# Transposing DMAs of the FFN issued by ScalarE, and the join of each chunk tied behind later work

## The chip, the cores and the metric

One core of a Trainium2 chip runs the program. Its engines are named as in the profile: PE (TensorE, matmul), PEld (TensorE's weight load), DVE (VectorE), ACT (ScalarE), POOL (GpSimd) and SP (SyncE, which here only issues DMAs). Each engine works through its own list of instructions in order and waits at semaphores for the others; ACT can issue DMAs too, on a queue of its own. The metric is the device time in microseconds (us) of one execution, lower is better; the median of 3 runs before is 962.99 us (962.33 to 964.85).

## What is computed

Two layers, each of FFN, mixer, FFN, with RMS norms around them, over 256 tokens of width 1024 in float32. The change touches the FFN alone, of which there are four.

```python
def _swiglu(h, w_in, w_out):
    gate, up = jnp.split(h @ w_in, 2, axis=-1)
    return (jax.nn.silu(gate) * up) @ w_out

def reference(x, ffn_w_in, ffn_w_out, norm_gains, mix_w_in, mix_w_out, ...):
    for l in range(DEPTH):
        g = norm_gains[l]
        h = _swiglu(_rmsnorm(x, g[0]), ffn_w_in[l, 0], ffn_w_out[l, 0])
        x = x + 0.5 * _rmsnorm(h, g[1])
        ...
        h = _swiglu(_rmsnorm(x, g[4]), ffn_w_in[l, 1], ffn_w_out[l, 1])
        x = x + 0.5 * _rmsnorm(h, g[5])
    return x
```

The hidden width 2816 is cut into 11 chunks (0 to 10) of 256.

## The kernel before

Products are made at float32 accuracy from three matmuls on rounded halves: a matrix is split into a high part (a copy rounded to fp32r) and a low part (the rest). Weights stream from HBM in pieces of 1 MB (tile `wr`, three buffers). Each half of a piece is cast by ACT (`wh`, L298) and subtracted by DVE (`wl`, L299); a load of the next piece can start when both halves of the piece in its buffer have been split. These two lines are most of what ACT and DVE do.

A plain chunk c of the FFN runs like this. Two pieces give the gate and up columns. PE multiplies them with the tokens' operands (`both`) into one PSUM bank for each of two token tiles (`pin` or `ptr`, in turn). ACT evacuates the gate half through silu (`sil`, L270), DVE multiplies it with the up half (`h`, L610). The output product needs the hidden values with the hidden index on the partitions, so they are transposed by a DMA: transposing DMAs work on 16-bit words, so ACT first copies the two 16-bit halves of each float apart (`planes`, L617), the DMA turns them (L619, issued by SP, written back over `h`), and DVE joins the halves again (`hT`, L625, the join). Then ACT and DVE split the joined values into `hh` and `hl` (L640, L641), and PE multiplies them with the chunk's third piece into the output banks (`bk`).

`STEPS` sets the order of the program: I is the input product of a chunk, O an output product, L a load of an output piece, S a part of the tokens' sums. The output product of chunk c stands behind the input product of chunk c + 1. P7 makes chunks 7 and 8 together with seven instead of eight products (`pair`, its two hidden tiles are `h` and `v`, each with its own planes and DMA). Chunk 9 is plain again. Chunk 10 is computed already turned (`in_turned`, L700 and L705; evacuated by `su`, L659 to L664, which ends in `hh` and `hl` of its own) and needs no DMA. The end of an FFN is then the output products of chunks 8, 9 and 10 (`END`), first for token tile 0, then for tile 1. So an FFN has ten transposing DMAs: seven for chunks 0 to 6, two for the pair, one for chunk 9.

The order in which the instructions of different steps stand on an engine is worked out by a scheduler while the program is built. It keeps dependences; `after(ins, others)` adds a tie, which makes an instruction stand behind others in that order without a semaphore, and `high_priority` moves work ahead. Waits at run time are for data and buffers alone, apart from that fixed order.

Of the kernel before, what the change touches and what calls it, by code (L numbers as in the profile page):

```python
# [19 lines left out]
U16 = mybir.dt.uint16  # L20
AF = mybir.ActivationFunctionType
ALU = mybir.AluOpType
# [6 lines left out]
NT = S // P  # L29
# [106 lines left out]
class _Trunk:  # L136
# [157 lines left out]
    def halved(self, raw):  # L294

        nc = self.nc
        lo, hi = self.half_tiles()
        ia = nc.scalar.activation(hi, raw, AF.Copy)  # L298
        iv = nc.vector.tensor_tensor(lo, raw, hi.bitcast(F32), op=ALU.subtract)  # L299
        for oa, ov in self.turns.pop(0) if self.turns else ():  # L300
            self.after(ia, [oa] if oa else [])
            self.after(iv, [ov] if ov else [])
        return hi, lo
# [303 lines left out]
    def ffn_hidden(self, pin, r, h):  # L607
        sil = self.t2("sil", (P, 256))
        self.func(sil, pin[:, 0:256], AF.Silu, scale=r)
        self.nc.vector.scalar_tensor_tensor(h, pin[:, 256:512], r, sil, op0=ALU.mult, op1=ALU.mult)  # L610

    def ffn_planes(self, h):


        nc = self.nc
        planes = self.t2("planes", (P, 2, 512), U16)
        nc.scalar.activation(planes, h.bitcast(U16).rearrange("p (n u) -> p u n", u=2), AF.Copy)  # L617
        turned = h.bitcast(U16).rearrange("p (b n) -> p b n", b=8)
        nc.sync.dma_start_transpose(turned, planes.rearrange("p u n -> p (u n)"))  # L619
        return turned  # L620

    def ffn_joined(self, turned):

        hT = self.t2("hT", (P, 2, 2, P))
        self.nc.vector.tensor_copy(hT.rearrange("p a b n -> p (a b n)").bitcast(U16).rearrange("p (n u) -> p u n", u=2),  # L625
                                   turned.rearrange("p (u b) n -> p u (b n)", u=2))
        return hT

    def ffn_split(self, hs):
# [47 lines left out]
    def ffn(self, pre, gi_post):  # L677
        xT, r = pre
# [26 lines left out]
                            self.nc.tensor.matmul(b[:, 0:NT * P], self.cols(w[kh], k)[1][:, c], both[kh][:, k, 0:NT].rearrange("p i t -> p (i t)"),  # L705
                                                  start=False, stop=kh == 1 and k == 3, skip_group_check=True)

        def ready(c, h):
            hT = self.ffn_joined(self.ffn_planes(h.rearrange("p t j -> p (t j)")))
            return self.ffn_split([hT[:, t] for t in range(NT)])  # L710

        def chunk(c, pins):
            h = self.t2("h", (P, NT, 256))
            for t in range(NT):
                self.ffn_hidden(pins[t], r[t], h[:, t])
            hs[c] = ready(c, h)

        def product(b, x, w, new):
            for k in range(4):
                for n, (st, mv) in enumerate(((x[0], 0), (x[0], 1), (x[1], 0))):  # L720
                    self.nc.tensor.matmul(b, st[:, k, :], self.cols(w, k)[mv], start=new and k == n == 0,  # L721
                                          stop=k == 3 and n == 2, skip_group_check=True)

        def pair(c):


            tt, stt = self.nc.vector.tensor_tensor, self.nc.vector.scalar_tensor_tensor
            w = self.pair_blocks()
            b1, b2, b3, b4 = self.bank_pin(), self.bank_pin(), self.bank_tr(), self.bank_tr()
            s1, s2, s3, s4 = sums  # L730
            ahead = self.tc.high_priority
            p1, sil, u, v, h0 = self.t2("p1"), self.t2("sil"), self.t2("u"), self.t2("v"), self.t2("h")
            product(b1, xT[0][0], w["P1"], True)
            with ahead():
                self.nc.scalar.activation(p1, b1, AF.Copy)
            product(b4, s1, w["P5"], True)
            product(b2, s2, w["P6"], True)
            with ahead():
                tt(u, b2, p1, op=ALU.subtract)
            product(b3, s3, w["P7"], True)  # L740
            with ahead():
                tt(v, u, b3, op=ALU.subtract)
                tt(v, v, b4, op=ALU.add)
            product(b1, xT[0][1], w["P2"], False)
            with ahead():
                self.func(sil, b1, AF.Silu, scale=r[0])
            product(b4, s4, w["P3"], False)
            with ahead():
                tt(h0, b4, u, op=ALU.add)
                stt(h0, h0, r[0], sil, op0=ALU.mult, op1=ALU.mult)  # L750
            with ahead():
                turned = [self.ffn_planes(h0)]
            product(b3, xT[1][1], w["P4"], False)
            with ahead():
                tt(u, b3, u, op=ALU.subtract)
                self.func(u, u, AF.Silu, scale=r[1])
                stt(v, v, r[1], u, op0=ALU.mult, op1=ALU.mult)
                turned.append(self.ffn_planes(v))
            hT = [self.ffn_joined(v) for v in turned]
            for j in range(2):  # L760
                hs[c + j] = self.ffn_split([h[:, j] for h in hT])

        hs, po, wo = {}, [], {}
        if not xT:

            xT += [[], []]
            pins = [self.bank_bk() for _ in range(NT)]
            self.piece_at = 2
            with self.tc.manual_schedule(engines={mybir.EngineType.PE, mybir.EngineType.Activation, mybir.EngineType.DVE}):
                self.first_chunk(pins, xT)  # L770
            self.turns = [[(self.cast, self.split)]]
            for t in range(NT):
                ss = self.small("ss", (P, 2))
                for hf in range(2):
                    self.after(self.square(t, hf, ss), [self.cast])
                r.append(self.rsqrt_sum(ss, EPS))
            chunk(0, pins)
            w1 = [self.piece(), self.piece()]
            wo[0] = self.piece()
            pins = [self.bank_pin() for _ in range(NT)]  # L780
            for kh in range(2):
                for t in range(NT):
                    in_piece(t, kh, pins[t], w1[kh])
            chunk(1, pins)
        else:

            w0 = [self.piece(), self.piece()]
            w1 = [self.piece()]
            pa, pa1 = self.bank_pin(), self.bank_pin()
            in_piece(0, 0, pa, w0[0])  # L790
            in_piece(0, 1, pa, w0[1])
            h = self.t2("h", (P, NT, 256))
            self.ffn_hidden(pa, r[0], h[:, 0])
            yield "second"
            in_piece(0, 0, pa1, w1[0])
            pb = self.bank_pin()
            in_piece(1, 0, pb, w0[0])
            in_piece(1, 1, pb, w0[1])
            yield "running"
            w1.append(self.piece())  # L800
            in_piece(0, 1, pa1, w1[1])
            self.ffn_hidden(pb, r[1], h[:, 1])
            hs[0] = ready(0, h)
            wo[0] = self.piece()
            pb1 = self.bank_pin()
            h = self.t2("h", (P, NT, 256))
            self.ffn_hidden(pa1, r[0], h[:, 0])
            in_piece(1, 0, pb1, w1[0])
            in_piece(1, 1, pb1, w1[1])
            self.ffn_hidden(pb1, r[1], h[:, 1])  # L810
            hs[1] = ready(1, h)
        both, swap = list(self.both), 0
        tokens = self.pair_tokens(both)
        for at, step in enumerate(STEPS):
            kind, c = step[0], int(step[1:])
            if kind == "P":
                pair(c)
            elif kind == "S":
                sums = next(tokens)
            elif kind == "L":  # L820
                if wo.get(c) is None:
                    wo[c] = self.piece()
            elif kind == "I":
                if c == 3:
                    g = self.load_gpost(gi_post)
                    yield "middle"
                ws = [self.piece(), self.piece()]
                for later in STEPS[at + 1:]:
                    if later[0] != "L":
                        break  # L830
                    wo[int(later[1:])] = self.piece()
                if c == END[-1]:
                    break
                pins = [self.bank_pin() if swap else self.bank_tr() for _ in range(NT)]
                swap = 1 - swap
                for kh in range(2):
                    for t in range(NT):
                        in_piece(t, kh, pins[t], ws[kh])
                chunk(c, pins)
            else:  # L840
                if not po:
                    po = [[self.bank_bk() for _ in range(2)] for _ in range(NT)]
                for t in range(NT):
                    out_part(c, t, hs[c], wo[c])
# [572 lines left out]
```

## Time and profile before

| | us |
|---|---|
| median of 3 runs | 962.99 |
| the profiled execution | 960.19 |
| span of the profiled execution, first to last instruction | 958.4 |
| lowest and highest of the 3 runs | 962.33, 964.85 |

| stretch of the profiled execution (us from the span's start) | what runs |
|---|---|
| 0 to 180 | FFN 1 of layer 1 |
| 180 to 290 | mixer of layer 1 |
| 290 to 475 | FFN 2 of layer 1, the second FFN of the four |
| 475 to 655 | FFN 1 of layer 2, the third |
| 655 to 765 | mixer of layer 2 |
| 765 to 958 | FFN 2 of layer 2, the fourth |

How to read the rows: a group of instructions has its line in the kernel, the engine, the operation, the tiles `out<-in` (buffer numbers left out), and the shapes. In the timeline a row begins with the start and the length in us; a bracket at the end is the time that the engine sat idle before, and what ended it. Matmuls overlap, so a row's length is not the spacing of matmuls; the difference of two starts is. A row of waits gives who waited for whom, the sum in us, how often and the longest. A row of windows gives the stretch, its length, and then the busy time of PE, PEld, DVE, ACT and POOL in it, each with the number of instructions, the granted clock of PE (1.00 is all of it), the busy share of the DMA engines and GB/s. DMA issues are not counted as busy time of the engine that issues them.

### The profile page before, as it was taken

What the parts mean: (1) busy time and instruction counts of PE and PEld (TensorE: products, weight loads), DVE (VectorE), ACT (ScalarE), POOL (GpSimd) and SP (SyncE); (2) the same over time, 40 slices, a digit from 0 to 9 for tenths busy, and PEclk for the clock granted to TensorE, in tenths of its full rate; (3) what the DMA queues carried; (4) which work ended last, traced back from release to release, by engine and by line L of the source; (5) the groups of instructions that cost most, each with busy time, mean ns of one, the idle gap of its engine ahead of it and who ended that gap; (6) DMA issues with size and microseconds to landing.
All of it is one profiled execution on the core that took longest, in us unless ns stands there. A gap on an engine that the chain in (4) does not pass through costs nothing.

```text
span 958.4 us, 12128 instructions
## 1 busy us (share of the span) xinstructions
PE 943.1 (98%) x4475; PEld 779.5 (81%) x4475; DVE 739.2 (77%) x1069; ACT 597.3 (62%) x973; POOL 30.2 (3%) x55
## 2 busy tenths in 40 slices
PE   9999999999999999999899999999999999999997
PEld 6888888888878888887788888888878888888885
DVE  7786986788858975786699669867888588759864
ACT  8666556578756755565476656664769466656652
POOL 2100000000010000000000000000000100000000
PEclk9999999999999999999999999999999999999999
DMA  8896477346342875467449663763454338754741
GB/s 309 277 305 233 138 280 209 129 138 239 142 163 91 307 244 189 147 256 211 181 147 306 187 219 139 291 204 133 173 200 147 118 132 273 275 193 142 271 119 45
DMA packets 69882, 189.34 MB, mean 198 GB/s; under 512 B 45274, under 2 KB 46426, under 8 KB 49086
## 3 DMA queue, kind: packets, MB, share of 16 engines
q1 hardware_dynamic: 69246, 187.95, 58.1%
q8 instruction: 35, 0.57, 0.2%
q10 hardware_dynamic: 576, 0.61, 0.2%
q14 instruction: 25, 0.20, 0.1%
HBM read 177.01 MB, written 1.05 MB: 186 GB/s over the span
## 4 chain that ended last, share of the span: by engine, by line
PE 84%; DVE 6%; ACT 4%; DMA 4%; issue 2%; POOLq 0%; ACTq 0%; DVEq 0%
PE pin L483 10%; PE pin L485 10%; PE pin L484 10%; PE bk L485 9%; PE bk L484 9%; PE bk L483 9%; PE ptr L484 5%; PE ptr L485 5%; PE ptr L483 5%; PE ptr L721 4%; DVE wl L299 3%; PE pin L721 3%; DMA wr<-in_w_dram 2%; ACT wh L298 2%; DMA h<-planes 2%
## 5 line engine op out<-in xcount | busy, mean ns | idle before, releaser
L299 DVE TENSOR_TENSOR wl<-wr,wh 128x1024 fp32r<-128x1024 f32 x324 | 388.0, 1219 | 82.1 <-ACT wh L298 81.1
L298 ACT ACTIVATE wh<-wr 128x1024 fp32r<-128x1024 f32 x324 | 331.5, 1054 | 130.7 <-DMA wr<-in_w_dram 60.6
L483 PE MATMUL pin<-wh,both 128*128 128x512 f32 x496 | 195.9, 396 | 0.0
L485 PE MATMUL pin<-wh,both 128*128 128x512 f32 x496 | 193.2, 390 | 0.0
L484 PE MATMUL pin<-wl,both 128*128 128x512 f32 x496 | 193.1, 390 | 0.0
L483 PE MATMUL bk<-wh,hh 128*128 128x512 f32 x352 | 135.3, 391 | 2.5 <-ACT hh L640 2.5
L484 PE MATMUL bk<-wl,hh 128*128 128x512 f32 x352 | 136.9, 389 | 0.0
L485 PE MATMUL bk<-wh,hl 128*128 128x512 f32 x352 | 135.0, 390 | 0.8 <-DVE hl L641 0.8
L485 PEld LDWEIGHTS pin<-wh,both 128*128 128x128 f32 x496 | 93.1, 188 | 19.8
L483 PEld LDWEIGHTS pin<-wh,both 128*128 128x128 f32 x496 | 93.3, 188 | 19.3 <-issue 0.7
L484 PEld LDWEIGHTS pin<-wl,both 128*128 128x128 f32 x496 | 93.3, 188 | 18.1
L483 PEld LDWEIGHTS bk<-wh,hh 128*128 128x128 f32 x352 | 66.1, 188 | 16.6 <-ACT hh L640 3.0
L485 PEld LDWEIGHTS bk<-wh,hl 128*128 128x128 f32 x352 | 66.1, 188 | 15.3 <-DVE hl L641 1.6
L484 PEld LDWEIGHTS bk<-wl,hh 128*128 128x128 f32 x352 | 66.1, 188 | 13.4
L484 PE MATMUL ptr<-wl,both 128*128 128x512 f32 x192 | 74.7, 389 | 0.0
L485 PE MATMUL ptr<-wh,both 128*128 128x512 f32 x192 | 74.7, 389 | 0.0
L483 PE MATMUL ptr<-wh,both 128*128 128x512 f32 x192 | 73.4, 389 | 0.0
L640 ACT ACTIVATE hh<-hT 128x256 fp32r<-128x256 f32 x80 | 29.1, 407 | 43.4 <-DVE hT L625 41.9
L625 DVE COPY hT<-h 128x1024 uint16<-128x1024 uint16 x36 | 27.3, 757 | 34.9 <-DMA h<-planes 34.9
L617 ACT ACTIVATE planes<-h 128x1024 uint16<-128x1024 uint16 x36 | 37.8, 1050 | 11.9 <-DVE h L610 11.9
L483 PEld LDWEIGHTS ptr<-wh,both 128*128 128x128 f32 x192 | 36.0, 188 | 7.5
L484 PEld LDWEIGHTS ptr<-wl,both 128*128 128x128 f32 x192 | 36.0, 188 | 7.5
(247 smaller groups left out, 1229.1 us busy)
## 6 DMA issues: line engine op xcount, KB each, us to landing
wr<-in_w_dram SPq DMA_DIRECT2D x162, 1024.0 KB, 5.0
gpost<-in_gpost_dram SPq DMA_DIRECT2D x6, 512.0 KB, 6.1
wr<-in_w_dram SPq DMA_DIRECT2D x2, 512.0 KB, 6.2
wr<-in_w_dram SPq DMA_DIRECT2D x3, 256.0 KB, 4.5
x<-in_x_dram SPq DMA_DIRECT2D x3, 256.0 KB, 4.9
h<-planes SPq DMA_TRANSPOSE x36, 4.7
out_dram<-x SPq DMA_DIRECT2D x2, 256.0 KB, 2.1
x<-in_x_dram SPq DMA_DIRECT2D x2, 128.0 KB, 3.0
```

The costliest lines, as they stand in the source:

```text
L298: ia = nc.scalar.activation(hi, raw, AF.Copy)
L299: iv = nc.vector.tensor_tensor(lo, raw, hi.bitcast(F32), op=ALU.subtract)
L483: mm(ps, xh, wh, start=start, stop=False)
L484: mm(ps, xh, wl, start=False, stop=False)
L485: mm(ps, xl, wh, start=False, stop=stop)
L617: nc.scalar.activation(planes, h.bitcast(U16).rearrange("p (n u) -> p u n", u=2), AF.Copy)
L625: self.nc.vector.tensor_copy(hT.rearrange("p a b n -> p (a b n)").bitcast(U16).rearrange("p (n u) -> p u n", u=2), turned.rearrange("p (u ...
L640: self.nc.scalar.activation(hh, h, AF.Copy)
L721: self.nc.tensor.matmul(b, st[:, k, :], self.cols(w, k)[mv], start=new and k == n == 0, stop=k == 3 and n == 2, skip_group_check=True)
```

## The change

Three things are changed in the FFN's code; nothing that is computed differs.

1. The transposing DMA (L619) is issued by ACT, on ACT's queue, instead of SP.
2. A chunk's planes and its DMA (`send`) are separated from its join and split (`ready`). The join of chunk c is written behind the evacuation of chunk c + 1 and tied to stand behind its first hidden multiply. For the chunk ahead of the pair the tie is to the pair's first subtraction (`u`).
3. The joins of the pair are tied to stand behind a DVE split of chunk 9's first weight piece (`cut`), and chunk 9's join behind one of chunk 10's first piece.

```diff
@@ halved
         iv = nc.vector.tensor_tensor(lo, raw, hi.bitcast(F32), op=ALU.subtract)
+        self.cut = iv
@@ ffn_hidden
-        self.nc.vector.scalar_tensor_tensor(h, pin[:, 256:512], r, sil, op0=ALU.mult, op1=ALU.mult)
+        return self.nc.vector.scalar_tensor_tensor(h, pin[:, 256:512], r, sil, op0=ALU.mult, op1=ALU.mult)
@@ ffn_planes
-        nc.sync.dma_start_transpose(turned, planes.rearrange("p u n -> p (u n)"))
+        nc.scalar.dma_start_transpose(turned, planes.rearrange("p u n -> p (u n)"))
@@ ffn_joined
-    def ffn_joined(self, turned):
+    def ffn_joined(self, turned, others=()):
...
+        self.after(i, others)
         return hT
@@ ffn
-        def ready(c, h):
-            hT = self.ffn_joined(self.ffn_planes(h.rearrange("p t j -> p (t j)")))
-            return self.ffn_split([hT[:, t] for t in range(NT)])
+        def send(c, h):
+            sent[c] = self.ffn_planes(h.rearrange("p t j -> p (t j)"))
+
+        def ready(c, others):
+            if c in sent:
+                hT = self.ffn_joined(sent.pop(c), others)
+                hs[c] = self.ffn_split([hT[:, t] for t in range(NT)])

         def chunk(c, pins):
             h = self.t2("h", (P, NT, 256))
-            for t in range(NT):
-                self.ffn_hidden(pins[t], r[t], h[:, t])
-            hs[c] = ready(c, h)
+            i = [self.ffn_hidden(pins[t], r[t], h[:, t]) for t in range(NT)]
+            send(c, h)
+            ready(c - 1, i[:1])
@@ pair
             with ahead():
-                tt(u, b2, p1, op=ALU.subtract)
+                i = tt(u, b2, p1, op=ALU.subtract)
+            ready(c - 1, [i])
...
-            hT = [self.ffn_joined(v) for v in turned]
+            sent["pair"] = c, turned
+
+        def pair_ready(others):
+            c, turned = sent.pop("pair")
+            hT = [self.ffn_joined(v, others) for v in turned]
             for j in range(2):
                 hs[c + j] = self.ffn_split([h[:, j] for h in hT])
@@ second to sixth phase, first chunks
-            hs[0] = ready(0, h)
+            send(0, h)
...
-            self.ffn_hidden(pb1, r[1], h[:, 1])
-            hs[1] = ready(1, h)
+            i = self.ffn_hidden(pb1, r[1], h[:, 1])
+            send(1, h)
+            ready(0, [i])
@@ steps, kind "I"
-                ws = [self.piece(), self.piece()]
+                ws = [self.piece()]
+                cut = self.cut
+                ws.append(self.piece())
+                if "pair" in sent:
+                    pair_ready([cut])
...
                 if c == END[-1]:
+                    ready(c - 1, [cut])
                     break
```

What follows are rows of the instruction order at the end of the second FFN, where chunks 7 to 10 finish. The numbers belong to buffers of that place; a tile has another number in the two programs when more tiles were named ahead of it. Tiles `h_3833` and `v_3832` (after: `h_3823` and `v_3822`) are the pair, `h_4102` is chunk 9, `su_4255` and `su_4268` are chunk 10.

ACT before, from the planes of the pair:

```order
L617 ACTIVATE planes_3913<-h_3833 128x1024
L617 ACTIVATE planes_3931<-v_3832 128x1024
L298 ACTIVATE wh_4159<-wr_4156 128x1024
L270 ACTIVATE sil_4103<-pin_4052,rs_560_2886 128x256
L298 ACTIVATE wh_4169<-wr_4166 128x1024
L298 ACTIVATE wh_4163<-wr_4156 128x1024
L640 ACTIVATE hh_3938<-hT_3934 128x256
L270 ACTIVATE sil_4106<-pin_4053,rs_585_2973 128x256
L650 ACTIVATE rows_4179<-ptr_4176 128x256
L640 ACTIVATE hh_3940<-hT_3936 128x256
L640 ACTIVATE hh_3946<-hT_3934 128x256
L640 ACTIVATE hh_3948<-hT_3936 128x256
```

ACT in the change, from the same planes:

```order
L618 ACTIVATE planes_3913<-h_3823 128x1024
L618 ACTIVATE planes_3931<-v_3822 128x1024
L620 DMA_TRANSPOSE h_3823<-planes_3913 128x8x128
L620 DMA_TRANSPOSE v_3822<-planes_3931 128x8x128
L270 ACTIVATE sil_4103<-pin_4052,rs_560_2886 128x256
L298 ACTIVATE wh_4153<-wr_4146 128x1024
L298 ACTIVATE wh_4159<-wr_4156 128x1024
L270 ACTIVATE sil_4106<-pin_4053,rs_585_2973 128x256
L652 ACTIVATE rows_4179<-ptr_4176 128x256
L298 ACTIVATE wh_4288<-wr_4281 128x1024
L642 ACTIVATE hh_4026<-hT_4022 128x256
L642 ACTIVATE hh_4028<-hT_4024 128x256
```

Before, casts of weights stand between the planes and the evacuations; in the change both planes are followed at once by the issues of both transposing DMAs, and the evacuation `sil_4103` of chunk 9's first bank stands behind the issues. The evacuation `sil_4106` stood behind `hh_3938`, which needs the pair's first join; now it stands ahead of the first `hh`.

DVE before, from the join of chunk 9:

```order
L625 COPY hT_4112<-h_4102 128x2x512
L641 TENSOR_TENSOR hl_4115<-hT_4112,hh_4114 128x256
L299 TENSOR_TENSOR wl_4172<-wr_4166,wh_4173 128x1024
L641 TENSOR_TENSOR hl_4117<-hT_4112,hh_4116 128x256
L299 TENSOR_TENSOR wl_4283<-wr_4281,wh_4284 128x1024
L299 TENSOR_TENSOR wl_4424<-wr_4422,wh_4425 128x1024
L660 TENSOR_TENSOR su_4255<-pin_4181,su_4255 128x256
L660 TENSOR_TENSOR su_4255<-pin_4182,su_4255 128x256
L661 TENSOR_TENSOR su_4255<-su_4255,rows_4179 128x256
L299 TENSOR_TENSOR wl_4428<-wr_4422,wh_4429 128x1024
L660 TENSOR_TENSOR su_4268<-ptr_4183,su_4268 128x256
L661 TENSOR_TENSOR su_4255<-su_4255,rows_4179 128x256
```

DVE in the change, from the same join:

```order
L626 COPY hT_4166<-h_4102 128x2x512
L299 TENSOR_TENSOR wl_4162<-wr_4156,wh_4163 128x1024
L643 TENSOR_TENSOR hl_4169<-hT_4166,hh_4168 128x256
L299 TENSOR_TENSOR wl_4283<-wr_4281,wh_4284 128x1024
L643 TENSOR_TENSOR hl_4171<-hT_4166,hh_4170 128x256
L299 TENSOR_TENSOR wl_4424<-wr_4422,wh_4425 128x1024
L299 TENSOR_TENSOR wl_4428<-wr_4422,wh_4429 128x1024
L662 TENSOR_TENSOR su_4255<-pin_4181,su_4255 128x256
L662 TENSOR_TENSOR su_4268<-ptr_4183,su_4268 128x256
L662 TENSOR_TENSOR su_4268<-ptr_4184,su_4268 128x256
L662 TENSOR_TENSOR su_4255<-pin_4182,su_4255 128x256
L299 TENSOR_TENSOR wl_4434<-wr_4432,wh_4435 128x1024
```

The join (`hT_4112`, after `hT_4166`) stands at the same place among DVE's work, ahead of the second split of chunk 9's output piece (4156, before 4166), those of pieces 4281 and 4422 and the sums of chunk 10. Right behind it now stands a weight split (`wl_4162`) that does not need it; the adds of chunk 10 stand together.

SP before, the loads and transposing DMAs at this place:

```order
L291 DMA wr_4042<-in_w_dram 128x2048
L291 DMA wr_4146<-in_w_dram 128x2048
L291 DMA wr_4156<-in_w_dram 128x2048
L291 DMA wr_4166<-in_w_dram 128x2048
L619 DMA_TRANSPOSE h_3833<-planes_3913 128x8x128
L619 DMA_TRANSPOSE v_3832<-planes_3931 128x8x128
L291 DMA wr_4281<-in_w_dram 128x2048
L291 DMA wr_4422<-in_w_dram 128x2048
L619 DMA_TRANSPOSE h_4102<-planes_4109 128x8x128
L291 DMA wr_4432<-in_w_dram 128x2048
```

SP in the change:

```order
L291 DMA wr_4042<-in_w_dram 128x2048
L291 DMA wr_4136<-in_w_dram 128x2048
L291 DMA wr_4146<-in_w_dram 128x2048
L291 DMA wr_4156<-in_w_dram 128x2048
L291 DMA wr_4281<-in_w_dram 128x2048
L291 DMA wr_4422<-in_w_dram 128x2048
L291 DMA wr_4432<-in_w_dram 128x2048
L291 DMA wr_4442<-in_w_dram 128x2048
```

The three transposing DMAs are gone from between the loads; the loads stand in the same order (pieces 4136, 4146 and 4156 of the change are 4146, 4156 and 4166 of before).

More of the change, by code (lines that the diff above doesn't have):

```diff
@@ L618, in ffn_planes @@
         turned = h.bitcast(U16).rearrange("p (b n) -> p b n", b=8)
-        nc.sync.dma_start_transpose(turned, planes.rearrange("p u n -> p (u n)"))
+        nc.scalar.dma_start_transpose(turned, planes.rearrange("p u n -> p (u n)"))
         return turned
-    def ffn_joined(self, turned):
+    def ffn_joined(self, turned, others=()):
         hT = self.t2("hT", (P, 2, 2, P))
-        self.nc.vector.tensor_copy(hT.rearrange("p a b n -> p (a b n)").bitcast(U16).rearrange("p (n u) -> p u n", u=2),
-                                   turned.rearrange("p (u b) n -> p u (b n)", u=2))
+        i = self.nc.vector.tensor_copy(hT.rearrange("p a b n -> p (a b n)").bitcast(U16).rearrange("p (n u) -> p u n", u=2),
+                                       turned.rearrange("p (u b) n -> p u (b n)", u=2))
+        self.after(i, others)
         return hT
@@ L758, in pair @@
                 turned.append(self.ffn_planes(v))
-            hT = [self.ffn_joined(v) for v in turned]
+            sent["pair"] = c, turned
+        def pair_ready(others):
+            c, turned = sent.pop("pair")
+            hT = [self.ffn_joined(v, others) for v in turned]
             for j in range(2):
                 hs[c + j] = self.ffn_split([h[:, j] for h in hT])
-        hs, po, wo = {}, [], {}
+        hs, po, wo, sent = {}, [], {}, {}
         if not xT:
```

## The prediction

> **What bounds the kernel now.** I read the page's busy shares first, then PE's own waits, then the windows round the four FFN ends, where this change works.
>
> ```profile
> PE 943.1 (98%) x4475; PEld 779.5 (81%) x4475; DVE 739.2 (77%) x1069; ACT 597.3 (62%) x973; POOL 30.2 (3%) x55
> PE bk L483 <- ACT hh L640: 2.5, 1, 2.5
> PE ptr L1039 <- DVE y L1302: 1.8, 2, 1.1
> PE ptr L1039 <- DVE ra L1224: 1.2, 1, 1.2
> PE ptr L700 <- ACT wh L298: 0.9, 1, 0.9
> PE bk L485 <- DVE hl L641: 0.8, 1, 0.8
> 126.00:176.00 50.00, 50.00 (x238) 41.91 (x237) 37.75 (x53) 30.48 (x45) 0.00 (x0) 1.00 0.75 245
> 423.00:473.00 50.00, 45.74 (x214) 37.44 (x213) 33.77 (x49) 27.05 (x42) 0.00 (x0) 1.00 0.76 237
> 600.00:651.00 51.00, 51.00 (x241) 42.52 (x240) 39.25 (x54) 30.86 (x44) 0.00 (x0) 1.00 0.72 246
> 892.00:942.00 50.00, 50.00 (x238) 41.93 (x237) 35.35 (x51) 27.41 (x41) 0.00 (x0) 1.00 0.52 167
> ```
>
> TensorE (PE) is busy almost without a break, at full granted clock. The waits of L1039 lie in the mixer, which the change leaves alone; the other three are all in one place, the end of the second FFN (423 to 473 us). The ends of the other three FFNs show PE busy 50.00 of 50.00, 51.00 of 51.00 and 50.00 of 50.00. So whatever DMA waits the change removes elsewhere, only the second FFN's end can pay. The matmuls there give the prize:
>
> ```profile
> 444.36 0.63 PE L700 MATMUL ptr<-both,wh 128*128 128x512 f32 x2
> 445.87 0.73 PE L700 MATMUL ptr<-both,wh 128*128 128x512 f32 x2 [0.88 <-ACT wh L298]
> 465.91 0.39 PE L484 MATMUL bk<-wl,hh 128*128 128x512 f32 x1
> 466.14 0.39 PE L485 MATMUL bk<-wh,hl 128*128 128x512 f32 x1
> 469.06 0.50 PE L483 MATMUL bk<-wh,hh 128*128 128x512 f32 x1 [2.53 <-ACT hh L640]
> 469.39 0.40 PE L484 MATMUL bk<-wl,hh 128*128 128x512 f32 x1
> 470.64 0.50 PE L485 MATMUL bk<-wh,hl 128*128 128x512 f32 x1 [0.85 <-DVE hl L641]
> ```
>
> Starts follow each other at 466.14 - 465.91 = 0.23 us when nothing is missing. Two from 444.36 should have been followed at 444.82, not 445.87 (1.05 lost); 466.14 by 466.37, not 469.06 (2.69); 469.39 by 469.62, not 470.64 (1.02). Together **4.76 us**: no gain beyond this is in sight, 0.5% of the run.
>
> What made them late? The chain of waits over 436 to 472 us, and ACT's and SP's rows there:
>
> ```profile
> 436.85 8.49 DMA h<-planes
> 451.28 5.90 DMA h<-planes
> 460.80 4.76 DMA wr<-in_w_dram
> 465.59 1.07 ACT wh L298
> 438.10 1.06 ACT L617 ACTIVATE planes<-v 128x1024 uint16<-128x1024 uint16 x1 [1.27 <-DVE v L757]
> 447.20 0.74 DVE L625 COPY hT<-v 128x1024 uint16<-128x1024 uint16 x1
> 450.20 1.06 ACT L617 ACTIVATE planes<-h 128x1024 uint16<-128x1024 uint16 x1 [0.24 <-DVE h L610]
> 457.27 0.76 DVE L625 COPY hT<-h 128x1024 uint16<-128x1024 uint16 x1 [4.97 <-DMA h<-planes]
> 458.15 0.42 ACT L640 ACTIVATE hh<-hT 128x256 fp32r<-128x256 f32 x1 [6.89 <-DVE hT L625]
> 462.58 0.63 ACT L659 ACTIVATE su<-pin 128x256 f32<-128x256 f32 x2
> 436.85 2.37 SPq L619 DMA_TRANSPOSE h<-planes  x1
> 439.56 4.05 SPq L619 DMA_TRANSPOSE v<-planes  x1
> 443.73 6.06 SPq L291 DMA_DIRECT2D wr<-in_w_dram  x2
> ```
>
> Chunk 9's transposing DMA lands 5.90 us after its issue. DVE's join (hT) stands there 4.97 us and ACT's hh behind it 6.89 us, each with weight splits queued behind it. Those splits free the buffer of a load, which starts only at 460.80 and lands 4.76 later, and the last chunk's su operations stand behind its split. Chunk 10 thus reaches PE 2.69 us late.
>
> **The change part by part.** (1) *Forty transposing DMAs go from SP to ACT.*
>
> ```profile
> L619 SPq DMA_TRANSPOSE h<-planes x36: 1231/1232/2696, 29.3 to 923.7; - x36
> L619 SPq DMA_TRANSPOSE v<-planes x4: 1232/1336/4055, 148.7 to 915.6; - x4
> DMA to landing us min/median/max: 2.7/4.8/8.5
> 320.00:370.00 50.00, 50.00 (x223) 41.38 (x222) 36.94 (x50) 31.38 (x43) 0.00 (x0) 1.00 0.76 247
> 25.00:65.00 40.00, 40.00 (x178) 33.14 (x177) 33.05 (x46) 28.52 (x42) 2.62 (x3) 1.00 0.89 288
> ACT wh L298 <- DMA wr<-in_w_dram: 8.7, 4, 2.6
> ```
>
> Each costs ACT an issue. No row shows a transpose issued by ACT; the nearest are SP's, 1.23 us at the median and 4.05 at the worst. I take 1.23: 40 x 1.23 = 49 us more on ACT, which was busy 597.3. Among plain chunks that is some 3 x 1.23 = 3.7 us in the 50 from 320 on, where ACT was busy 31.4 and PE never waited: hidden, costing nothing while ACT stays well under 50. In the crowded first part (25 to 65 us) ACT goes from 28.5 to about 32 of 40; it had waited 8.7 us for weights between 30 and 60, and that idle time covers the issues. Without such cover one issue in front of a cast costs up to 1.23.
>
> (2) *SP is rid of them.* At 436.85 and 439.56 they held SP's queue for 2.37 and 4.05 us, and the load behind left at 443.73. Loads now leave as their buffers come free. Where PE had no wait that buys nothing; at the second FFN's end it takes the late weights away.
>
> (3) *Landing.* A transpose no longer stands behind an earlier load in SP's queue, but loads may now overtake it. Bounds: 2.7 to 8.5 us from issue; I take the median, 4.8.
> The Trainium skill (DMA: Bandwidth & Descriptors, Queues, rings and completion order) says that each DMA engine takes turns between the queues that have work, a packet at a time; the row of 8.49 us, a transpose issued while loads were landing, fits standing behind them, and by that rule a transpose on a queue of its own would land nearer 2.7, all 4.76 would go, and the sum would be -4.3 where the median gives -3.5. The same page (Rules for kernel authors) says that spreading DMAs over issuing engines brings no bandwidth, it only saves issue time; by that the landing would stay at 5.90, which the third rival below prices.
>
> (4) *The joins are tied later.* Chunk c's join (0.76) and split now follow the next chunk's evacuation. Its product is a whole chunk further on, so on PE's path this costs nothing. While the join waits for nothing, DVE's weight splits no longer queue behind a landing. The last ones can't be moved so far: chunks 7 and 8 are tied to a weight split of chunk 9, chunk 9 to one of chunk 10, and all three are needed at the end.
>
> (5) *The second FFN's end, step by step.* planes of v still ends at 438.10 + 1.06 = 439.16. ACT then issues h (to 440.4) and v (to 441.6), so h leaves 2.3 us later than before. v, issued at 440.4, lands at 445.2, its join stood at 447.20: 2.0 sooner. Chunk 9's planes move from 450.20 to some 448.2 and end at 449.3; DMA of 4.8: 454.1, against 457.2. In the new DVE order the second half of that chunk's weights is split right behind the join, so the load behind it can leave at 454.1 + 0.76 + 1.22 = 456.1 instead of 460.80, and lands at 460.8 instead of 465.56. From that landing to PE's 469.06 it took 3.5 us: 464.3. The su operations can't begin before their banks: 462.58 less the lost 1.05 is 461.5 at the latest, and the fourth FFN shows their length without a late load:
>
> ```profile
> 933.87 0.38 ACT L659 ACTIVATE su<-pin 128x256 f32<-128x256 f32 x1 [3.25 <-PE pin L705]
> 938.34 0.51 ACT L640 ACTIVATE hh<-su 128x128 fp32r<-128x128 f32 x2 [1.85 <-PE bk L484]
> ```
>
> There 938.34 - 933.87 - 1.85 of waiting for a bank = 2.6 us to hh, or 4.5 with it. So hh is ready between 464.3 and 466.0, and PE without its first loss wants it at 466.37 - 1.05 = 465.32. Left over: 0 to 0.7, and up to the 1.02 of hl. With a transpose of 2.7 all 4.76 go; with 8.5 each way none do. I take **-4.0**.
>
> (6) *The other ends.* The third FFN has the same order, planes of h and v ahead of both issues; its h leaves later, its v about when it did. The first and fourth keep h's issue ahead of v's planes, with two weight casts now between planes and issue of v. I allow **+0.5** for one of them to reach PE; 0 if shorter landings cover it, some 2 if not.
>
> Sum: -4.0 + 0.5 = -3.5 us. The profiled execution took 960.19 (span 958.4 and 1.8 around it): 956.7. The median of the runs shown is 962.99, 2.8 above it, so the forecast in those terms is **959.5**.
>
> **The rivals.**
> *A: the wait only changes its name* (0.25). Something else of the same chain, say the weight split that now stands ahead of the su products in DVE's order, keeps chunk 10 as late as it was, or small stalls at the other ends give the gain back. For it: all of DVE's work there is still there, and the third end has no margin that I can show. Against: 5 us of DVE idle time stood in that chain. Time: 963, 961 to 965.
> *B: slower, ACT is held by its own issues* (0.14). In the second and third FFN two transposes stand back to back on ACT. If the second blocks, as SP's did (4.05), ACT's evacuations, which SP's hold never touched, stand still for 2.37 + 4.05 - 2 x 1.23 = 4.0 us more than I counted. It decides where v's issue takes over some 3 us, because the banks' evacuation and chunk 9's planes follow it directly. The second FFN then gains nothing, the third loses up to 4.0: 963.0 + 4.0 = 967. Against it: SP's queue was full of loads then, ACT's holds transposes alone.
> *C: nothing lands sooner* (0.11). Loads run ahead on SP's queue and share the DMA engines, which were 0.76 busy at that end. With 5.90 for chunk 9 in place of 4.8 the chain of (5) ends 1.1 later, hh at 465.4 to 467.1: 0.1 to 1.7 left over and the 1.02 of hl, so a gain of 2.0 to 3.6, less the 0.5: about 960.7.
>
> **How the numbers follow.** Forecast 0.50, A 0.25, B 0.14, C 0.11. The forecast's own range is 958.0 to 961.0 (4.76 gone and nothing new: 958.2; 2 left over: 961). A difference under about 0.3% (2.9 us) can't be told from none with a few runs. Faster by more: most of the forecast's half and a little of C, 0.47. Within: the rest of it, C and A's most, 0.40. Slower: B less its mild end, 0.13. The range runs from 957.5 (all of the prize, and a little from runs that waited longer than the profiled one) to 966.0, which leaves out B's far end and little of A.
>
> **What would show it.** Right: PE's waits for hh L640, hl L641 and wh L298 at 440 to 475 us fall from 4.3 to under 1; PE stays busy throughout at the other three ends; SP no longer shows issues of 2 to 4 us; the last join waits under 4 us; ACT's issues take about 1.23. Wrong: an issue of 3 us or more on ACT ahead of sil or planes; new PE waits for wh, wl or hh at 25 to 65 us, in the pair, or at the third end; landings over 6 us at the median. What would also upset it is that the unprofiled runs lose time elsewhere: they are 2.8 above the profiled one, and if that lies in DMA waits the gain could be larger.

## The result, and the profile after

The changed kernel takes 991.93 us (median of 6 runs, 985.66 to 1006.89) against 962.83 before (also of 6 runs by now): the ratio is 1.0304, 95% interval 1.0252 to 1.0356. One of the six runs, 1006.89, lies over 1.5% above the fastest of them and is left out of the ratio. The change is slower by 3%, far above the range of the prediction (957.5 to 966.0). The profiled execution took 992.38, its span is 990.5: 32.1 more than before.

From the page of the changed kernel, the busy times, and from its waits of PE and DVE (sum in us, how often, the longest):

```profile
PE 953.4 (96%) x4475; PEld 786.0 (79%) x4475; DVE 738.8 (75%) x1069; ACT 598.1 (60%) x973; POOL 29.1 (3%) x55
PE bk L484 <- ACT hh L642: 22.6, 5, 9.9
DVE hT L626 <- DMA h<-planes: 55.8, 9, 12.6
```

PE's wait for `hh`, 2.5 us in one place before, is now 22.6 in five, and behind it stand DVE's joins, waiting 55.8 us for transposing DMAs in 9 places (34.9 in 23 before). PE is also busy 10.3 us longer (953.4 against 943.1) with the same matmuls. So of the 32.1 us, 21.8 are more idle time and 10.3 longer matmul time. The transposes themselves, from the view of the tile `planes` (issue time in ns min/median/max, first and last start):

```profile
L620 ACTq DMA_TRANSPOSE h<-planes x36: 1247/1249/3355, 31.1 to 955.6; - x36
L620 ACTq DMA_TRANSPOSE v<-planes x4: 1249/1813/4497, 162.4 to 939.4; - x4
DMA to landing us min/median/max: 2.7/6.5/19.3
```

The median landing went from 4.8 to 6.5 us, the worst from 8.5 to 19.3. All four FFN ends now lose time, and so does the first FFN's beginning, where PE had never waited. First that place, in windows (stretch, length, busy time of PE, PEld, DVE, ACT and POOL, granted clock, DMA share, GB/s):

```profile
35.00:40.00 5.00, 5.00 (x24) 4.13 (x22) 3.98 (x6) 4.04 (x7) 1.59 (x3) 1.00 1.12 184
40.00:45.00 5.00, 1.75 (x8) 1.13 (x6) 0.00 (x0) 0.00 (x0) 0.00 (x0) 1.00 1.21 131
45.00:50.00 5.00, 0.00 (x0) 0.00 (x0) 0.00 (x0) 0.00 (x0) 0.00 (x0) 0.70 0.87 217
50.00:55.00 5.00, 3.39 (x8) 2.71 (x9) 4.63 (x10) 3.86 (x7) 0.00 (x0) 0.50 0.41 121
55.00:60.00 5.00, 5.00 (x18) 3.96 (x18) 5.00 (x8) 4.67 (x7) 0.00 (x0) 0.77 0.70 249
37.00:38.00 1.00, 1.00 (x6) 0.81 (x6) 1.00 (x3) 0.78 (x2) 0.87 (x2) 1.00 0.06 25
43.00:44.00 1.00, 0.00 (x0) 0.00 (x0) 0.00 (x0) 0.00 (x0) 0.00 (x0) 1.00 0.06 25
44.00:45.00 1.00, 0.00 (x0) 0.00 (x0) 0.00 (x0) 0.00 (x0) 0.00 (x0) 1.00 0.05 19
```

From 42 to 50 us none of the five engines does anything. At 37 to 38, and again at 43 to 45, the DMA engines, with transposes and loads outstanding, move 19 to 25 GB/s (bytes count in the window in which their packet starts), against 184 over the whole of 35 to 40 us. The packet records say what stands: from 43.3 to 44.9 us, 16 load packets of 8 KB are in flight; 15 of them are the same throughout (2.4 to 5.5 us each), and the rest of the traffic is one transposing packet of 256 bytes (0.018 us) and one 8 KB packet (0.309 us) in turns, every 0.32 us. The clock then falls to half. The timeline of ACT, SP, DVE and PE at this place, with two rows of SP before at the end, tells who waits for what:

```profile
31.06 1.33 ACTq L620 DMA_TRANSPOSE h<-planes  x1
38.37 3.35 ACTq L620 DMA_TRANSPOSE h<-planes  x1
51.14 0.72 ACT L642 ACTIVATE hh<-hT 128x256 fp32r<-128x256 f32 x2 [11.88 <-DVE hT L626]
27.79 0.33 SPq L291 DMA_DIRECT2D wr<-in_w_dram  x1
31.55 5.65 SPq L291 DMA_DIRECT2D wr<-in_w_dram  x2
50.37 0.74 DVE L626 COPY hT<-h 128x1024 uint16<-128x1024 uint16 x1 [11.39 <-DMA h<-planes]
41.36 0.39 PE L486 MATMUL ptr<-wh,both 128*128 128x512 f32 x1
51.61 0.79 PE L484 MATMUL bk<-wh,hh 128*128 128x512 f32 x1 [9.87 <-ACT hh L642]
52.20 0.63 PE L485 MATMUL bk<-wl,hh 128*128 128x512 f32 x1
52.63 0.63 PE L484 MATMUL bk<-wh,hh 128*128 128x512 f32 x1
29.34 1.34 SPq L619 DMA_TRANSPOSE h<-planes  x1
30.78 0.52 SPq L291 DMA_DIRECT2D wr<-in_w_dram  x1
```

ACT issues chunk 0's transpose at 31.06. The load that stood right behind it on SP's queue before (30.78 behind 29.34, the last two rows) now leaves at 27.79, 3.3 us ahead of it, and SP issues the next one at 31.55 and one more at 36.88. The first packet of the transpose starts at 34.9. It lands 19.3 us after its issue, the join starts at 50.37, `hh` at 51.14, and PE goes on at 51.61, 10.25 us after 41.36. Its matmuls then start 0.43 us apart (52.20, 52.63) where 0.23 is usual: a stall costs a second time through the clock. The trace's clock record has half clock for 23.9 us while the program runs; PE is busy for 17.7 of them, so about 8.8 of the 10.3 us can come from it (an estimate, half of 17.7). Where the other 1.5 come from is not shown. The four FFN ends, in windows:

```profile
140.00:190.00 50.00, 47.35 (x219) 39.53 (x218) 32.28 (x43) 27.86 (x38) 0.00 (x0) 0.97 0.70 214
437.00:492.00 55.00, 51.16 (x239) 42.02 (x238) 40.23 (x57) 31.34 (x48) 0.00 (x0) 1.00 0.71 244
620.00:675.00 55.00, 51.70 (x236) 42.75 (x235) 38.55 (x55) 30.45 (x45) 0.00 (x0) 0.97 0.67 229
920.00:960.00 40.00, 33.96 (x144) 27.84 (x143) 21.60 (x27) 18.39 (x25) 0.00 (x0) 0.91 0.74 177
```

PE misses 2.7, 3.8, 3.3 and 6.0 us there, in three of them with a lower clock. Before, only the second end missed any (4.26 of 50 us).

### The profile page after: what moved, and what is told of

It is laid out like the page before. It is cut to its first block, busy times and chain, and to the rows that moved or that the text cites. A ratio compares the mean times of both kernels' runs of the same rounds, so it can differ in the third digit from the quotient of the medians.

```text
span 990.5 us, 12070 instructions
## 1 busy us (share of the span) xinstructions
PE 953.4 (96%) x4475; PEld 786.0 (79%) x4475; DVE 738.8 (75%) x1069; ACT 598.1 (60%) x973; POOL 29.1 (3%) x55
## 3 DMA queue, kind: packets, MB, share of 16 engines
q10 hardware_dynamic: 42816, 11.11, 7.8%
## 5 line engine op out<-in xcount | busy, mean ns | idle before, releaser
L484 PE MATMUL bk<-wh,hh 128*128 128x512 f32 x352 | 139.6, 399 | 22.6 <-ACT hh L642 22.6
L485 PE MATMUL bk<-wl,hh 128*128 128x512 f32 x352 | 139.0, 396 | 0.0
L484 PEld LDWEIGHTS pin<-wh,both 128*128 128x128 f32 x496 | 93.3, 188 | 19.3 <-issue 0.7
L485 PEld LDWEIGHTS bk<-wl,hh 128*128 128x128 f32 x352 | 67.6, 192 | 13.7
L486 PE MATMUL ptr<-wh,both 128*128 128x512 f32 x192 | 74.7, 389 | 0.0
L484 PE MATMUL ptr<-wh,both 128*128 128x512 f32 x192 | 73.4, 389 | 0.0
L626 DVE COPY hT<-h 128x1024 uint16<-128x1024 uint16 x36 | 27.0, 750 | 55.8 <-DMA h<-planes 55.8
L727 PE MATMUL ptr<-wh,both 128*128 128x512 f32 x128 | 42.0, 389 | 0.0
```

Source lines behind the costliest of these rows:

```text
L484: mm(ps, xh, wh, start=start, stop=False)
L485: mm(ps, xh, wl, start=False, stop=False)
L486: mm(ps, xl, wh, start=False, stop=stop)
L626: i = self.nc.vector.tensor_copy(hT.rearrange("p a b n -> p (a b n)").bitcast(U16).rearrange("p (n u) -> p u n", u=2), turned.rearrange("p ...
```

## The experiments

After the result, theory **M** was: a transpose on a queue of its own moves beside the loads, and each holds the other up. Its rivals: **J**, the later joins leave their products too little slack; **A**, ACT is held by its own 40 issues; **R**, loads run ahead on SP's queue, now that no transpose stands between them. An edit of one line also lets the scheduler place other work anew: read from the traces, some 50 of ACT's 973 and 70 of DVE's 1069 operations stand elsewhere in e2 than in the change. So a difference of a few us is not pinned to an edit. The results of all runs:

| kernel | median us | ratio to before (95%) | landing us min/median/max | load packets over 2 us, longest us |
|---|---|---|---|---|
| before | 962.83 | | 2.7/4.8/8.5 | 0, 1.76 |
| the change | 991.93 | 1.0304 (1.0252 to 1.0356) | 2.7/6.5/19.3 | 69, 6.33 |
| e1 queue only | 1013.82 | 1.0534 (1.0490 to 1.0579) | 2.7/5.9/20.0 | 54, 7.59 |
| e2 joins only | 963.04 | 0.9999 (0.9986 to 1.0012) | 2.7/4.7/7.7 | 0, 1.70 |
| e3 e2 with ACT busier | 961.45 | 0.9982 (0.9969 to 0.9996) | 2.7/4.5/7.6 | 0, 1.59 |
| e4 2 KB load packets | 1022.34 | 1.0626 (1.0561 to 1.0690) | 2.7/8.3/13.5 | 0, 1.92 |
| e5 fence | 965.20 | 1.0032 (1.0005 to 1.0060) | 2.7/4.1/7.5 | 2, 2.25 |
| e6 plain copy | 962.53 | 1.0003 (0.9986 to 1.0020) | 2.2/5.7/7.8 | 0, 1.76 |
| e7 first one on SP | 995.54 | 1.0340 (1.0287 to 1.0393) | 2.7/6.1/18.4 | 62, 6.72 |
| e8 e2 with 2 KB packets | 978.71 | 1.0175 (1.0147 to 1.0204) | 2.7/4.9/8.2 | 1, 2.14 |
| e9 leave behind | 982.35 | 1.0175 (1.0127 to 1.0222) | 2.7/4.1/13.7 | 39, 4.32 |
| e10 fence, old joins | 980.03 | 1.0169 (1.0120 to 1.0218) | 2.7/4.5/8.0 | 1, 2.21 |
| e11 short plain copy | 965.38 | 1.0042 (1.0024 to 1.0060) | 2.2/4.8/9.3 | 0, 1.76 |

The last column is counted in the packet records of each profiled execution's trace: of the packets of 2 KB and more on SP's queue (23,268, of which 20,736 have 8 KB, median 0.309 us; in e4 and e8 85,476, nearly all of 2 KB), those that took over 2 us. In the change all 69 are of 8 KB.

### Which half of the change: e1, e2, e3

e1 is the kernel before with one line changed, e2 the change with that line put back:

```diff
-        nc.sync.dma_start_transpose(turned, planes.rearrange("p u n -> p (u n)"))
+        nc.scalar.dma_start_transpose(turned, planes.rearrange("p u n -> p (u n)"))
```

> The kernel before with one edit: ACT issues the transposing DMAs; the joins stand where they stood before. Theory M (a transpose on a queue of its own moves beside the loads, each holding the other up): landings as in the change, median 6 to 7 us and a worst one of 15 or more, and since the joins now stand even earlier in DVE's order, the time is as slow as the change or slower, 985 to 1005. Rival J (the later joins leave their products too little slack): the joins are back at their old places, so the time falls to 960 to 970. Rival A (ACT is held by its own 40 issues): as slow as the change, 985 to 1000, whatever the landings are.

> The change with one edit: SP issues the transposing DMAs again; the joins stay tied as in the change. M: landings as before (median near 4.8, worst under 10), no PE gap of 10 us at 40, clock 1.00 there, 957 to 965. J: as slow as the change, 980 to 1000. A: ACT is rid of its issues, 957 to 965; this run alone does not tell M from A.

e3 is e2 with work for ACT behind each transpose:

```diff
         nc.sync.dma_start_transpose(turned, planes.rearrange("p u n -> p (u n)"))
+        for u in range(2):
+            nc.scalar.activation(self.junk_tile(), planes[:, u], AF.Copy)
```

> The run with SP's transposes and tied joins, and behind each issue two dead casts on ACT (128x512 each, some 0.55 us by half of the 1.06 of the planes' cast, so 1.1 us for each of 40 transposes, near the 1.23 of an issue). A: the load on ACT is back, so the time is near the change, 980 to 1000. M and J's opposite: ACT has room, the time stays within 3 us of the run without the dead casts.

e1 is even slower than the change and than M had it (985 to 1005), 1013.82; e2 equals the kernel before within 0.14%. J falls: with the landings of SP's queue the ties cost nothing. The waits of DVE's joins in e1, e2 and before, in this order:

```profile
DVE hT L625 <- DMA h<-planes: 116.1, 29, 17.3
```

```profile
DVE hT L626 <- DMA h<-planes: 21.8, 8, 5.8
```

```profile
DVE hT L625 <- DMA h<-planes: 34.9, 23, 5.5
```

The ties take 13.1 us of waiting off DVE in e2 (34.9 - 21.8), and with bad landings they save 22 us (1013.82 to 991.93). But with transposes on SP's queue PE does not wait for that time anyway. From the view of line 622 in e3:

```profile
L622 ACT ACTIVATE junk<-planes x80: 610/616/633, 28.3 to 922.9; 128x512 bf16<-128x512 uint16 x80
```

Eighty dead casts of 0.616 us, 1.23 per transpose, just what an issue takes, cost nothing (961.45): A falls as far as the ordinary issue time is meant; e5 below, with all 40 issues on ACT, costs 0.3%. An issue that blocks for 3 to 4.5 us is not tried by this, but the loss does not need one: the longest issue on ACT is 2.58 us in both e1 and e4, which are slower than the change.

### Packets in turns: e4, e8

e4 is the change, e8 is e2, both with every load cut into four:

```diff
-        self.load = nc.sync.dma_start(raw.rearrange("p a b -> p (a b)"), self.a["w"][i])
+        for k in range(4):
+            c = slice(k * 512, k * 512 + 512)
+            self.load = nc.sync.dma_start(raw.rearrange("p a b -> p (a b)")[:, c], self.a["w"][i][:, c])
```

> The change, with each weight load of 128 rows of 8 KB cut into four loads of 128 rows of 2 KB on the same queue. M, if the two queues' packets take turns one by one: a transpose's packet waits behind a quarter of the bytes, its landing beside loads falls (median towards 4, worst under 10), and most of the 29 us goes: 960 to 975. M, if transposes and loads hold each other up whatever the packet's size: landings and time about as in the change, 980 to 1000. J and A: no change from the change, 985 to 1000.

> A control for the run with cut loads: transposes on SP's queue and tied joins, with each weight load cut into four of 2 KB rows. If cutting costs nothing by itself, 960 to 966, and the slowness of the run with cut loads (1022) lies in the two queues. If the cut loads themselves are slow or late, 975 to 1000, and that run says nothing of turns between packets.

e4 got slower still, 1022.34, above every branch of what was expected. The control shows that cutting costs by itself: 978.71 - 963.04 = 15.7 us. Beyond that the queue of its own costs 1022.34 - 978.71 = 43.6 us with 2 KB packets, against 28.9 with 8 KB ones (991.93 - 963.04). So a shorter packet of the loads does not help: no load packet took over 2 us in e4 and the worst landing fell from 19.3 to 13.5, but the median rose from 6.5 to 8.3.

### Ahead or beside: e5, e9, e10

In e5 and e9 the transposes stay on ACT's queue, and the load that stood right behind transpose n in SP's queue in e2 (a table, BEHIND, names it; 38 of the 40 have one) waits: in e5 for the landing, in e9 for a tiny cast on ACT right behind the issue. e10 is e5 with the joins of the kernel before, and a table taken from that kernel.

```diff
         self.load = nc.sync.dma_start(raw.rearrange("p a b -> p (a b)"), self.a["w"][i])
+        for n in [n for n, j in enumerate(BEHIND) if j == i]:
+            self.tc.add_manual_dep(self.load.ins, self.sent[n].ins.name, mybir.DependencyInfo(
+                mybir.DependencyClass.Sync, mybir.DependencyReason.DATA), reason="landing")
...
-        nc.scalar.dma_start_transpose(turned, planes.rearrange("p u n -> p (u n)"))
+        self.sent = getattr(self, "sent", []) + [nc.scalar.dma_start_transpose(turned, planes.rearrange("p u n -> p (u n)"))]
```

and in e9, in place of the last line:

```diff
+        i = nc.scalar.dma_start_transpose(turned, planes.rearrange("p u n -> p (u n)"))
+        with self.tc.high_priority():
+            mark = nc.scalar.activation(self.junk_tile()[:, 0:1], planes[:, 0, 0:1], AF.Copy)
+        self.after(mark, [i])
+        self.sent = getattr(self, "sent", []) + [mark]
```

> The change (transposes on ACT's queue), but the load that stood right behind a transpose in SP's queue when SP issued both now waits for that transpose's landing. No load can overtake a transpose any more; loads that left ahead of it are still moving beside it. If the harm comes from loads that overtake (theory R): landings fall to about those of SP's queue (median under 5, worst under 9) and the time to 960 to 972. If it comes from the loads that were under way already (theory M in its narrow form): landings stay at a median of 6 or more, the first gap stays near 10 us, and the time stays at 985 to 1005. Between the two: both share in it.

> As the run with the fence, but the load waits only until ACT has issued the transpose (for a 128x1 dead cast that stands right behind the issue), not until it has landed. The load can no longer run ahead, but it moves beside the transpose. If the harm is loads that move beside a transpose (theory M): landings with a worst one of 12 or more, dozens of held load packets, and the time goes back towards the change, 978 to 1000. If the harm was that loads ran ahead on SP's queue (theory R): as with the fence, 960 to 970, worst landing under 9.

> The kernel before with transposes on ACT's queue and the same fence: the load that stood right behind a transpose in SP's queue waits for its landing; the joins stand where they stood before. Without the fence this was 1013.8. If late landings are all that is wrong, 962 to 972, as with the fence and tied joins (965.2), and the ties are worth nothing again. If the old joins suffer from something else on ACT's queue, over 980.

The fence takes back 26.7 of the 29.1 us (991.93 to 965.20), and landings are better than on SP's queue. With the load let go at the issue 17.2 of them are lost again (982.35). The intervals of the three do not overlap. By these differences both count: that loads run ahead of a waiting transpose (some 10 us, e9 against the change), and that they move beside a moving one (some 17, e5 against e9). The split is rough. In e9 loads still run ahead of some transposes: at the third FFN's end ACT issues `h` at 630.56 and `v` at 631.88, SP issues the load let go by `h` at 632.09, its packets start at 633.05, and the first of `v` at 635.75. And the profiled executions lie closer together than the medians (972.29 in e5, 977.02 in e9). The packet records tell the two apart more directly. Taken in order, 1024 packets to a transpose (rough where two are on the way at once), the forty need these times in all:

| | issue to first packet, us | first to last packet, us |
|---|---|---|
| before | 90 | 70 |
| the change | 102 | 117 |
| e5 fence | 78 | 76 |
| e9 leave behind | 78 | 85 |

Most of what the change adds is time in which a transpose moves, not time in which it waits to begin. The transposes' row and PE's largest wait in e9, then the window of that wait:

```profile
DMA to landing us min/median/max: 2.7/4.1/13.7
PE pin L710 <- DVE h L615: 9.1, 2, 8.1
637.00:638.00 1.00, 0.00 (x0) 0.00 (x0) 0.00 (x0) 0.00 (x0) 0.00 (x0) 1.00 3.32 337
638.00:639.00 1.00, 0.00 (x0) 0.00 (x0) 0.00 (x0) 0.00 (x0) 0.00 (x0) 1.00 0.40 89
639.00:640.00 1.00, 0.00 (x0) 0.00 (x0) 0.00 (x0) 0.00 (x0) 0.00 (x0) 1.00 0.37 121
```

The median landing is as with the fence (4.1); what differs is the worst ones. Here `v`, issued at 631.88, lands 11.7 us later; DVE stands at its join, the `h` that PE waits for stands behind it, and the DMA engines slow down as in the change, though less far. A few landings make the time there, not the typical one.

e10 missed its first branch by 8 us, at the edge of the second: with good landings (worst 8.0) the old joins still leave it at 980.03. From its waits:

```profile
DVE hT L629 <- DMA h<-planes: 47.0, 25, 7.2
PE bk L487 <- ACT hh L644: 12.1, 4, 5.1
```

Joins that stand early wait 47.0 us in 25 places, and 12.1 of it reaches PE. Why this is so much more than the 34.9 and 2.5 of the kernel before, at landings that look alike, stays open; no run here tells the later loads from the place of the joins.

### One landing alone: e7

```diff
-        nc.scalar.dma_start_transpose(turned, planes.rearrange("p u n -> p (u n)"))
+        q = nc.scalar if getattr(self, "begun", False) else nc.sync
+        self.begun = True
+        q.dma_start_transpose(turned, planes.rearrange("p u n -> p (u n)"))
```

> The change, with only the first of the 40 transposes (issued near 31 us, landed 19.3 us later in the change) back on SP's queue. M: the gap of 10 us at 41 and the clock drop behind it go, about 12 to 13 us of the 29: 976 to 983; the gaps at the ends of the FFNs stay. If the time is not made of such single landings, it stays at 988 to 996.

A miss: 995.54, no gain. PE's longest waits in e7:

```profile
PE bk L484 <- ACT hh L644: 19.8, 5, 11.8
PE pin L485 <- DVE wl L299: 5.7, 1, 5.7
```

PE's gap at 40 us shrank from 9.9 to 1.7 us, but others grew: 5.7 at 55 us and 11.8 at 164 us, the first FFN's end, where the change had 2.7. Which transpose is caught depends on where the loads happen to be; the loss is not a property of one of them.

### Transposing, or any copy: e6, e11

e6 puts a plain DMA in the place of each transposing one, e11 two plain DMAs of alternate blocks, which make the same 40,960 packets of 256 bytes as the transposes (counted in the trace). First e6, then e11:

```diff
-        nc.scalar.dma_start_transpose(turned, planes.rearrange("p u n -> p (u n)"))
+        nc.scalar.dma_start(turned.rearrange("p b n -> p (b n)"), planes.rearrange("p u n -> p (u n)"))
```

```diff
-        nc.scalar.dma_start_transpose(turned, planes.rearrange("p u n -> p (u n)"))
+        flat = planes.rearrange("p u n -> p (u n)")
+        for j in range(2):
+            nc.scalar.dma_start(turned.rearrange("p (k j) n -> p j k n", j=2)[:, j], flat.rearrange("p (k j n) -> p j k n", k=4, j=2)[:, j])
```

> The change, with a plain DMA of the same 256 KB on ACT's queue in the place of each transposing one; the hidden values are then not transposed, so the output products compute something else. 128 rows of 2 KB take the place of 1024 packets of 256 bytes. If what suffers beside the loads is the many small packets of a transpose (M with turns by packet): landings fall to 2 to 4 us, PE's gap at 40 us goes, 958 to 970. If anything on a second queue suffers beside the loads: landings of 5 to 7 us and 980 or more.

> As the run with plain copies on ACT's queue, but each copy is made in two DMAs, one of the even and one of the odd blocks of 256 bytes, so that it moves in 1024 packets of 256 bytes, as many and as short as a transpose's; the hidden values are again not transposed, so the output products compute something else. If short packets beside 8 KB loads are the harm (theory M with turns by packet): worst landing of 12 or more and 980 to 1005. If it is the transposing itself beside the loads: landings within 2 us of the plain copy's (2.2 to 7.8), no load packet held for over 2 us, 958 to 968.

The same bytes over the same queue at the same places cost nothing as plain copies (962.53), and next to nothing in packets of 256 bytes (965.38). The queue and landing rows of e11 and a window of it, then the landing row of e6 and its window 37 to 38, where the DMA engines nearly stood still in the change:

```profile
q10 hardware_dynamic: 42816, 11.11, 5.1%
DMA to landing us min/median/max: 2.2/4.8/9.3
43.00:44.00 1.00, 1.00 (x6) 0.84 (x5) 0.90 (x3) 1.00 (x2) 0.00 (x0) 1.00 0.96 401
```

```profile
DMA to landing us min/median/max: 2.2/5.7/7.8
37.00:38.00 1.00, 1.00 (x6) 0.82 (x5) 1.00 (x2) 0.52 (x2) 0.00 (x0) 1.00 0.99 418
```

The number of packets on ACT's queue (42,816) is that of the change; their time is 5.1% of the DMA engines' against 7.8%. Neither run has a load packet of over 2 us. Nor is it that the plain copies met fewer loads. The time in which packets of transposes (or copies) were in flight, and how much of it load packets were too:

| | in flight, us | with loads, us | load packets over 2 us |
|---|---|---|---|
| before | 70.1 | 32.1 | 0 |
| e5 fence | 74.4 | 33.9 | 2 |
| e9 leave behind | 76.9 | 41.5 | 39 |
| the change | 96.8 | 62.7 | 69 |
| e6 plain copy | 73.3 | 55.1 | 0 |
| e11 short plain copy | 85.2 | 54.8 | 0 |

So M holds in a narrower form than it was stated: what suffers, and makes the loads suffer, is a *transposing* DMA that moves while loads of another queue move. Not the queue, not the bytes, not their cut into short packets. What it is in the transposing, say where its packets are written, no run here shows.

## Why the prediction was wrong, point by point

- *What bounds the kernel* was read rightly: PE, with 4.76 us to be won at the second FFN's end and nothing elsewhere. What was missed is the other direction: the other ends were at 50.00 of 50.00 with the order on SP's queue, and the change gives that up (with it, e2 misses 0.9 us at the third end and nothing at the first and fourth).
- *(1) ACT's issues*: 1.23 us each was right (1.249 measured), and e3 shows that this is hidden. Five took 2.0 to 4.5 us, the longest for `v` at the third FFN's end, as rival B had feared; no run isolates their price.
- *(2) Loads leave as their buffers come free, which buys nothing where PE had no wait*: it buys nothing and costs. The load at 27.79 that now leaves 3.3 us ahead of the transpose of 31.06, and the one at 31.55 right behind it, are the plainest case; holding such loads back (e5) recovers 26.7 us.
- *(3) Landing* is the step that failed. It was bounded by 2.7 and 8.5 us, from rows in which transposes and loads shared one queue and moved together for less time (32.1 us, against 62.7 in the change). The step did say that loads may now overtake, but gave that no price outside SP's range. Measured: median 6.5 (over 6 was among its signs of being wrong), worst 19.3, and the loads held with it. The median was the wrong number too: e6 has a median of 5.7 and e9 one of 4.1; the first costs nothing, the second 19 us. The Trainium skill's rule (DMA: Bandwidth & Descriptors, Queues, rings and completion order), turns between queues by packet, was read there as a landing near 2.7. The trace does not agree with that reading: the median is 6.5, and 4.8 for plain packets of the same size (e11). Turns as such do show, 256 bytes against 8 KB every 0.32 us from 43.3 to 44.9 us, but with 15 other load packets standing still meanwhile; in e11 the same mix moved at 401 GB/s.
- *(4) The joins tied later* cost nothing on PE's path: right, by e2 (0.9999). They also bring nothing while the landings are good.
- *(5) The second FFN's end*: the gain of 4.0 did not come, because it rested on (3). In e2, where landings are as before, PE's lost starts there fell from 4.8 to 2.8 us, but 1.1 us came up at the third end, and the time is unchanged.
- *(6) Other ends, +0.5*: the windows of the three ends miss 2.7, 3.3 and 6.0 us, with the lower clock on top, and the first FFN's beginning, for which no term stood, lost 9.9 and a slow stretch behind it. Again this is (3).
- *The rivals*: B had the right sign and not the cause (e1 and e4 lose more without an issue over 2.58 us). C had the cause in its first half (loads run ahead and share the DMA engines), but priced it as 1.1 us on one landing, without a tail, at the one place where PE waited already. The price of a late landing in a place without a wait before, and of the clock that falls after a stall (about 8.8 us, the estimate above), was in no rival.

## What to carry to other kernels

A queue is also an order. Where a transposing DMA and large loads share one, the loads behind a transpose come after it; before it is moved to a queue of its own, ask which loads will then move beside it, and do not bound its landing by rows of the shared queue alone. When joins wait in an engine's list of work, look at the worst landing and what stands behind it, not at the median. If a transpose must be on another engine's queue, let the loads behind it wait until it has landed. Here that came within 0.3% of the kernel before with the later joins (e5), and within 1.7% with the early ones (e10).

No version here beats the kernel before by more than 0.3%; e3, at 0.9982 (0.9969 to 0.9996), is nearest, and a gain of that size, with dead casts and another order of the work, is no reason to prefer it.

## What the runs showed of the hardware

- A transposing DMA on ACT's queue beside loads on SP's can bring the 16 DMA engines nearly to a standstill for 1 to 2 us (19 to 25 GB/s), with single 8 KB packets of the loads held for up to 6.33 us (7.59 in e1) against a median of 0.309. While 15 of them stood, one more place went on, a packet of each in turns every 0.32 us. On one queue none took over 1.76 (before, e2, e3), and plain copies on the second queue do not do it (1.76 in e6 and e11). How the two block each other inside the DMA engines is not shown by any run.
- PE stood still from 41.7 us on; at 47.0, after 5.3 us, the granted clock fell to half and stayed there until some 57 us: windows of 0.70, 0.50 and 0.77, and matmuls 0.43 us apart. It fell again, for 3.4 us, after stalls of 2.7 us at the first FFN's end and 2.0 at the third's (0.97 in both windows), but not after one of 2.7 at the second's (1.00). So the length of a stall alone does not tell here whether the clock falls.
